# A hybrid decoder layer on one Trainium2 core: one layout for the low parts of the held weights, and two more warm-up matmuls

## The chip, the core and the metric

The kernel runs on one core of a Trainium2 chip. The core has five engines that work side by side: TensorE (matmuls; the profile calls it PE, and its weight loads PEld), VectorE (DVE), ScalarE (ACT), GpSimd (POOL) and SyncE (SP, which issues most of the DMAs). The metric is the time of one execution on the device in microseconds. Before the change it is 1077.86 us, the median of three runs (1077.21 to 1078.08).

## The reference

One decoder layer on x of 256 tokens by 2048 channels, all in float32. Cut to what carries the work:

```python
def reference(x, pre_mix_g, w_in, b_forget, sinks, grp_swa_g, grp_fox_g, w_out, post_mix_g,
              pre_ffn_g, w_up, conv_w, conv_b, w_down, post_ffn_g):
    h = rmsnorm(x, pre_mix_g)
    proj = h @ w_in                                   # 2048 -> 4368
    q_a, k_a, v_a, q_b, k_b, v_b, f_b = split(proj)
    o_a = swa_sink_attention(q_a, k_a, v_a, sinks)    # window 128, 16 heads, 2 kv heads, ALiBi
    log_f = log_sigmoid(f_b + b_forget)
    o_b = forgetting_attention(q_b, k_b, v_b, log_f)  # 16 heads, decay from cumsum(log_f)
    mix = concat([rmsnorm(o_a, grp_swa_g), rmsnorm(o_b, grp_fox_g)]) @ w_out   # 2048 -> 2048
    x = x + rmsnorm(mix, post_mix_g)
    h = rmsnorm(x, pre_ffn_g)
    u = causal_dwconv(h @ w_up, conv_w, conv_b)       # 2048 -> 2 * 5632, width 3
    gate, val = split(u)
    y = (gelu(gate) * val) @ w_down                   # 5632 -> 2048
    return x + rmsnorm(y, post_ffn_g)
```

## The kernel before

Every large product is made from split numbers. A float32 weight goes into a high part (a copy in the type that TensorE takes at full rate, `whi`, made by ScalarE on L128) and a low part (the rest, `wlo`, made by VectorE on L131); the activations are split in the same way. A product is then high by high, high by low and low by high. The activations lie transposed in `hT`: for each of 16 slices of 128 channels, 256 columns of high parts and 256 of low parts, side by side. So one matmul of a high weight with all 512 columns makes two of the three products, and a second of the low weight with the 256 high columns makes the third.

Weights come in units: a **unit** is four slices of 128 rows by 256 columns, 512 KB, loaded by one DMA of SyncE into one of five `raw` buffers, and split into one of five pairs of `whi` and `wlo` buffers (`w_parts`, `w_split`, `w_high`). The `wlo` buffer is 128 floats longer than a unit, and a held unit's low part begins at a multiple of 16 bytes inside it. Where it begins is taken from a table: `at = row[unit[0] % len(row)] * 4` floats, so 2 stands for 32 bytes, 4 for 64, 14 for 224. In the kernel before, the row is (2, 4) for everything ahead of w_up, and in the w_up projections row `LOW[place[0]]`, another one for each projection.

`proj_T` makes one projection of 256 output columns, in two banks of PSUM: 16 slices by two banks, so 32 high matmuls of 128x512 (L274) and 32 low ones of 128x256 (L281). Its runs say in which order the units go. In w_in it has four runs: units 0 and 1 high, 0 and 1 low, 2 and 3 high, 2 and 3 low; there are 11 such projections (queries and keys). In w_up it has three (LONG): units 0 and 1 high, all four low, 2 and 3 high; there are 43 of these, 21 in the first half of the feed-forward stage and 22 in the second, each half followed by its share of w_down (L296). The first gate projection of w_up is written out by itself in `first_gate`, with units that `gate_unit` splits ahead of time while the output projection still runs. Attention is woven into the w_in projections: `later(n, f)` queues its pieces, and each run's `tick()` calls those that are due.

TensorE's instructions go in the order in which they are written. The other engines' order is set by the tile framework's scheduler, save where `keep_in_program_order` or a manual schedule holds it. At the head of the program x and the first weights come in pieces: two loads of 256 KB of x, each followed by half of the first w_in unit, and then alternating units of w_in and of x. Six matmuls on a zeroed tile (`warm_up`, L183) run while the first data is under way; then a transpose of a gain vector (L189), the transposes of x's first two slices (L321, `x_part`), those of the next two, and the first matmuls of w_in (L235 high, L240 low, `unit_T`).

Of the kernel before, what the change touches and what calls it, by code (L numbers as in the profile page):

```python
# [24 lines left out]
NEG = -1e30  # L25
FHALF = 22
HOLD = 6
LOW = (
# [9 lines left out]
)  # L38
ROOM = 112


# [1 line left out]
def hybrid_layer(ctx: ExitStack, tc: tile.TileContext, x, pre_mix_g, w_in, b_forget, sinks,  # L43
# [17 lines left out]
    def bank(tag="acc"):  # L61
        return ps.tile([P, 512], F32, tag=tag, bufs=4, name="bank_" + tag)
# [4 lines left out]
    def tick():  # L67
        now[0] += 1
        for f in todo.pop(now[0], []):
            f()  # L70
# [8 lines left out]
    def w_load(src, a, c, pin=False):  # L79
        raw = wp.tile([P, UNIT], F32, tag="raw", bufs=5, name="raw")  # L80
        i = sp.dma_start(raw[:, :a * c].rearrange("p (a c) -> p a c", a=a), src)
        if pin:
            tc.keep_in_program_order(i)
        return raw, a, c

    place, unit = [-1], [0]

    def w_parts(n, keep=None, held=True):

        if keep and keep[0] is None:  # L90
            return keep[1]
        where, pre, nb = (keep[0], "h", keep[1]) if keep else (wp, "w", WB)
        hi = where.tile([P, UNIT], F32R, tag=pre + "hi", bufs=nb, name="whi")
        if where is not wp:
            lo = where.tile([P, UNIT], F32R, tag=pre + "lo", bufs=nb, name="wlo")
            return hi[:, :n], lo[:, :n]
        lo = where.tile([P, UNIT + 128], F32R, tag=pre + "lo", bufs=nb, name="wlo")
        at = 0
        if held:
            row = (2, 4) if place[0] < 0 else LOW[place[0]]  # L100
            at = row[unit[0] % len(row)] * 4
            unit[0] += 1
        return hi[:, :n], lo[:, at:at + n]

    def w_high(unit, keep=None, held=True):

        raw, a, c = unit
        n = a * c
        hi, lo = w_parts(n, keep, held)
        act.copy(hi, raw[:, :n])  # L110

        def low():
            dve.tensor_tensor(lo, raw[:, :n], hi.bitcast(F32), op=ALU.subtract)

        return [x.rearrange("p (a c) -> p a c", a=a) for x in (hi, lo)], low

    def w_split(unit, pin=False, keep=None, begun=None, between=None,
                held=True):

        raw, a, c = unit  # L120
        n = a * c
        hi, lo = begun or w_parts(n, keep, held)
        for i in range(2 if between else 1):
            cs = slice(i * 512, i * 512 + 512) if between else slice(0, n)
            if i:
                between()
            if not between or i:
                i1 = act.copy(hi[:, cs], raw[:, cs])  # L128
                if pin:
                    tc.keep_in_program_order(i1)  # L130
            i2 = dve.tensor_tensor(lo[:, cs], raw[:, cs], hi[:, cs].bitcast(F32), op=ALU.subtract)  # L131
            if pin:
                tc.keep_in_program_order(i2)
        return [x.rearrange("p (a c) -> p a c", a=a) for x in (hi, lo)]
# [4 lines left out]
    def w_rows(w, k0, a, c0, c):  # L139
        return w[k0 * P:(k0 + a) * P, c0:c0 + c].rearrange("(a p) c -> p a c", p=P)  # L140
# [40 lines left out]
    def warm_up(n):  # L181
        for i in range(n):
            pe.matmul(warm, junk[:, 0:P], junk, start=True, stop=True)  # L183
# [17 lines left out]
    def to_T(srcs, t0, n, g0, pin=False):  # L201

        for part in range(2):
            for kt, tb in srcs:
                hi = hT[:, kt, t0:t0 + n]
                gk = gcol[:, g0 + kt:g0 + kt + 1]
                if part == 0:
                    i = act.activation(hi, tb, AF.Copy, scale=gk)
                else:
                    i = dve.scalar_tensor_tensor(hT[:, kt, 256 + t0:256 + t0 + n], tb, gk,  # L210
                                                 hi.bitcast(F32), op0=ALU.mult, op1=ALU.subtract)
                if pin:
                    tc.keep_in_program_order(i)
# [43 lines left out]
    def proj_T(w, c0, banks, runs=((0, 1), (0, 1), (2, 3), (2, 3))):  # L257

        parts, last = {}, ((len(runs) - 1) % 2, KT - 1)
        unit[0] = 0  # L260
        if len(runs) == 3:
            place[0] += 1

        def get(u):
            if u not in parts:
                parts[u] = w_split(w_load(w_rows(w, u * 4, 4, c0, 256), 4, 256))
            return parts[u]

        def high(u):
            hi = get(u)[0]  # L270
            for a in range(4):
                kt = u * 4 + a
                for m, b in enumerate(banks):
                    pe.matmul(b, hi[:, a, m * P:(m + 1) * P], hT[:, kt, 0:512], start=(kt == 0),  # L274
                              stop=(last == (0, kt)))

        def low(u):
            lo = get(u)[1]
            for a in range(4):
                for m, b in enumerate(banks):  # L280
                    pe.matmul(b[:, 256:512], lo[:, a, m * P:(m + 1) * P],  # L281
                              hT[:, u * 4 + a, 0:256], start=False,
                              stop=(last == (1, u * 4 + a)))

        for n, us in enumerate(runs):
            for u in us:
                (low if n % 2 else high)(u)
                tick()
# [13 lines left out]
    with tc.tile_pool(name="mixp", bufs=1) as mp:  # L302
# [10 lines left out]
        def x_part(c, k2s, tag="att"):  # L313
            srcs = []
            for k2 in k2s:
                for j in range(2):
                    if tag == "acc" or j == 0:
                        tb = bank(tag)
                    kt = c * 4 + k2 * 2 + j
                    for t in range(2):  # L320
                        pe.transpose(tb[:, j * 256 + t * P:j * 256 + (t + 1) * P],  # L321
                                     x_in[:, t, kt * P:(kt + 1) * P], ident)
                    srcs.append((kt, tb[:, j * 256:(j + 1) * 256]))
            to_T(srcs, 0, 256, 0, True)
# [25 lines left out]


        begun = w_parts(UNIT)
        tc.keep_in_program_order(dve.tensor_copy(begun[0][:, 0:512], head[:, 0:512]))
        x_part(0, (0,), "acc")
        bkv = [bank("att"), bank("att")]
        bq0 = [bank(), bank()]
        for u in range(4):
# [244 lines left out]
        for g in range(4):  # L602
            if g == 0:
                b2 = bq0
            else:
                b2 = [bank(), bank()]
                proj_T(w_in, g * 256, b2)
            for m in range(2):
                swa_pair(2 * g + m, q_pair(b2[m]), stages(6 + 8 * (2 * g + m) - 8 * g))
# [60 lines left out]
        for g in range(4):  # L670
            bq = [bank(), bank()]
            proj_T(w_in, 1280 + g * 256, bq)
            qs = [q_pair(b) for b in bq]
            bk = [bank(), bank()]
            proj_T(w_in, 2304 + g * 256, bk)
            for m in range(2):
                ki = (2 * g + m + 2) % NK
                k_pair(bk[m], ki)
                fox_pair(2 * g + m, qs[m], ki, stages(3 + 8 * m))
# [111 lines left out]
                pieces.append(out_cols(2, 0, whole))  # L791
        gate = []

        def gate_unit(u):
            (hi, lo), low = w_high(w_load(w_rows(w_up, u * 4, 4, 0, 256), 4, 256))
            gate.extend((hi[:, i, :], lo[:, i, :]) for i in range(4))
            return low

        gate_unit(0)()
        evac_b(0, 3, out_cols(3, 0, whole))  # L800
        mix_rstd(0)
        lows = [gate_unit(u) for u in (1, 2, 3)]
        for n in range(4):
            residual(0, n)
# [254 lines left out]
```

## Time and profile before

| | |
|---|---|
| median of three runs | 1077.86 us (1077.21 to 1078.08) |
| the profiled execution | 1078.04 us |
| its span, first to last instruction | 1076.3 us |
| instructions | 16263 |
| matmuls on TensorE | 5986 |
| read from memory, written | 199.58 MB, 2.11 MB: 187 GB/s over the span |
| high matmuls of `proj_T` (L274) | 1088 + 640 |
| low matmuls of `proj_T` (L281) | 1088 + 640 |

A page of the profile gives busy time, share of the span and count for each engine, the chain of work that ended last (followed back from the last instruction, at each step to what released it), and groups of instructions with their busy time, the mean length of one in ns, and the idle time ahead of them. A row of the chain or of the timeline begins with the start in us from the beginning of the span and the length in us; `x16` at its end is the number of instructions merged into it. A matmul's record runs to the end of its drain, which overlaps the next one, so what one costs is the distance between starts.

### The profile page before, as it was taken

What the parts mean: (1) busy time and instruction counts of PE and PEld (TensorE: products, weight loads), DVE (VectorE), ACT (ScalarE), POOL (GpSimd) and SP (SyncE); (2) the same over time, 40 slices, a digit from 0 to 9 for tenths busy, and PEclk for the clock granted to TensorE, in tenths of its full rate; (3) what the DMA queues carried; (4) which work ended last, traced back from release to release, by engine and by line L of the source; (5) the groups of instructions that cost most, each with busy time, mean ns of one, the idle gap of its engine ahead of it and who ended that gap; (6) DMA issues with size and microseconds to landing.
All of it is one profiled execution on the core that took longest, in us unless ns stands there. A gap on an engine that the chain in (4) does not pass through costs nothing.

```text
span 1076.3 us, 16263 instructions
## 1 busy us (share of the span) xinstructions
PE 1064.7 (99%) x5986; PEld 927.6 (86%) x5986; DVE 735.3 (68%) x1200; ACT 613.2 (57%) x1060; POOL 225.2 (21%) x252
## 2 busy tenths in 40 slices
PE   9999999999999999999999999999999999999996
PEld 7889988888889888888888888888888888888886
DVE  5978877776568876777777444457777777765563
ACT  6766766667557755655555443446555555644450
POOL 3343333332022211212121000002121211201111
PEclk9999999999999999999999999999999999999998
DMA  8745666544863766666665666666666666665652
GB/s 282 222 123 153 181 183 204 166 160 150 296 224 110 231 195 195 193 180 197 192 187 187 198 196 194 195 193 186 185 199 186 191 193 193 192 198 190 192 169 79
DMA packets 164970, 202.88 MB, mean 188 GB/s; under 512 B 6780, under 2 KB 130972, under 8 KB 164380
## 3 DMA queue, kind: packets, MB, share of 16 engines
q1 hardware_dynamic: 164176, 201.27, 60.7%
q8 instruction: 47, 0.77, 0.3%
q10 hardware_dynamic: 716, 0.58, 0.2%
q14 instruction: 31, 0.25, 0.1%
HBM read 199.58 MB, written 2.11 MB: 187 GB/s over the span
## 4 chain that ended last, share of the span: by engine, by line
PE 95%; DVE 2%; DMA 1%; POOL 1%; ACT 1%; issue 0%; SPq 0%; DVEq 0%; POOLq 0%; ACTq 0%
PE bank_acc L296 35%; PE bank_acc L274 21%; PE bank_att L274 14%; PE bank_acc L281 11%; PE bank_att L281 7%; PE bank_att L461 1%; PE bank_att L496 1%; PE bank_att L505 1%; PE bank_att L235 1%; PE bank_acc L235 1%; DVE wlo L131 0%; PE bank_att L507 0%; DMA x_in<-in_x_dram 0%; PE bank_att L240 0%; DVE hT L754 0%; DMA cb<-c_dram 0%
## 5 line engine op out<-in xcount | busy, mean ns | idle before, releaser
L131 DVE TENSOR_TENSOR wlo<-raw,whi 128x1024 fp32r<-128x1024 f32 (+3 forms) x357 | 432.5, 1220 | 243.8 <-ACT whi L128 233.0
L128 ACT CAST whi<-raw 128x1024 fp32r<-128x1024 f32 (+3 forms) x356 | 363.6, 1034 | 274.9 <-issue 130.1
L274 PE MATMUL bank_acc<-hT,whi 128*128 128x512 f32 x1088 | 259.5, 391 | 0.0
L274 PEld LDWEIGHTS bank_acc<-hT,whi 128*128 128x128 f32 x1088 | 200.6, 188 | 39.8
L296 PE MATMUL bank_acc<-whi,G 128*128 128x512 f32 (+1 forms) x724 | 214.6, 378 | 0.0
L863 POOL TENSOR_TENSOR u<-u,rowf 128x256 f32<-128x256 f32 x88 | 97.6, 1131 | 496.7 <-DVE u L862 494.4
L296 PEld LDWEIGHTS bank_acc<-whi,G 128*128 128x128 f32 x724 | 133.7, 188 | 25.6
L274 PE MATMUL bank_att<-hT,whi 128*128 128x512 f32 x640 | 150.6, 390 | 0.0
L274 PEld LDWEIGHTS bank_att<-hT,whi 128*128 128x128 f32 x640 | 118.7, 188 | 23.9
L281 PE MATMUL bank_acc<-hT,wlo 128*128 128x256 f32 x1088 | 138.7, 281 | 0.0
L281 PEld LDWEIGHTS bank_acc<-hT,wlo 128*128 128x128 f32 x1088 | 134.8, 188 | 4.1
L296 PE MATMUL bank_acc<-wlo,G 128*128 128x512 f32 (+1 forms) x362 | 137.0, 379 | 0.0
L296 PE MATMUL bank_acc<-whi,oT 128*128 128x512 f32 (+1 forms) x272 | 82.5, 380 | 0.0
L281 PEld LDWEIGHTS bank_att<-hT,wlo 128*128 128x128 f32 x640 | 77.9, 188 | 1.7
L296 PEld LDWEIGHTS bank_acc<-wlo,G 128*128 128x128 f32 x362 | 68.1, 188 | 12.7
L281 PE MATMUL bank_att<-hT,wlo 128*128 128x256 f32 x640 | 78.3, 280 | 0.0
L296 PEld LDWEIGHTS bank_acc<-whi,oT 128*128 128x128 f32 x272 | 50.2, 188 | 9.3
L296 PE MATMUL bank_acc<-wlo,oT 128*128 128x512 f32 (+1 forms) x136 | 51.2, 377 | 0.0
L296 PE MATMUL bank_acc<-whi,hT 128*128 128x384 f32 (+1 forms) x192 | 47.6, 324 | 0.0
L865 ACT ACTIVATE yg<-u,cw 128x256 f32<-128x256 f32 x44 | 26.5, 602 | 28.8 <-POOL u L863 28.8
L865 ACT ACTIVATE yv<-u,cw 128x256 f32<-128x256 f32 x44 | 26.5, 603 | 27.0 <-POOL u L863 27.0
L479 ACT ACTIVATE p<-p,nm 128x256 f32<-128x256 f32 (+1 forms) x64 | 28.4, 445 | 20.5 <-DVE nm L467 20.4
(200 smaller groups left out, 1013.1 us busy)
## 6 DMA issues: line engine op xcount, KB each, us to landing
raw<-in_w_up_dram SPq DMA_DIRECT2D x176, 512.0 KB, 3.7
raw<-in_w_down_dram SPq DMA_DIRECT2D x88, 512.0 KB, 4.6
raw<-in_w_in_dram SPq DMA_DIRECT2D x51, 512.0 KB, 4.6
raw<-in_w_out_dram SPq DMA_DIRECT2D x32, 512.0 KB, 4.5
raw<-in_w_in_dram SPq DMA_DIRECT2D x16, 384.0 KB, 3.7
cb<-c_dram SPq DMA_DIRECT2D x8, 256.0 KB, 3.1
x_sb<-in_x_dram SPq DMA_DIRECT2D x2, 1024.0 KB
raw<-in_w_in_dram SPq DMA_DIRECT2D x5, 408.0 KB, 3.5
```

Of the source, the lines that this page charges most:

```text
L128: i1 = act.copy(hi[:, cs], raw[:, cs])
L131: i2 = dve.tensor_tensor(lo[:, cs], raw[:, cs], hi[:, cs].bitcast(F32), op=ALU.subtract)
L235: pe.matmul(b, hi[:, a, m * P:(m + 1) * P], hT[:, kt, 0:512], start=(kt == 0), stop=(kt == KT - 1))
L274: pe.matmul(b, hi[:, a, m * P:(m + 1) * P], hT[:, kt, 0:512], start=(kt == 0), stop=(last == (0, kt)))
L281: pe.matmul(b[:, 256:512], lo[:, a, m * P:(m + 1) * P], hT[:, u * 4 + a, 0:256], start=False, stop=(last == (1, u * 4 + a)))
L296: pe.matmul(b, a, r[:, cols], start=(first and i == 0), stop=(last and i == 2))
L461: pe.matmul(sb[e][:, cs], a[r, t * P:(t + 1) * P], b[r, 0:nk], start=(n == 0), stop=(n == 2))
L479: act.activation(p[:, e, cs], p[:, e, cs], AF.Exp, bias=nm[:, t, e:e + 1], scale=-1.0, accum_out=rs[:, t, e:e + 1])
L496: pe.transpose(pb[:, i * P:(i + 1) * P], p[:, e, c:c + P], ident)
L505: pe.matmul(ov, values(hl, 0), p[:, :, 0:256], start=(n == 0), stop=False)
L863: pool.tensor_tensor(u[:, 2:258], u[:, 2:258], rowf, op=ALU.mult)
L865: act.activation(y, u[:, 2:258], AF.Identity, bias=cw[:, 3, ch:ch + 1], scale=cw[:, 2, ch:ch + 1])
```

## The change

The table of 43 rows becomes one row, (14, 4, 4, 4): 224, 64, 64 and 64 bytes for the four units of every projection of three runs. Projections of four runs take the first two entries in turn: 224, 64, 224, 64. So do the units at the head of the program. Ahead of the first gate's units the count is set to zero and the period to four, so these too are at 224, 64, 64, 64 (they were at 32, 64, 32, 64). The buffers and their sizes stay, and no instruction of the splitting moves. On TensorE two more warm-up matmuls stand behind the first four transposes of x.

```diff
-LOW = (
-    (2, 0, 0, 0), (2, 1, 1, 1), (2, 2, 2, 2), (2, 3, 3, 3), (2, 4, 4, 4),
-    (2, 5, 5, 5), (2, 6, 6, 6), (2, 8, 8, 8), (2, 10, 10, 10), (2, 12, 12, 12),
-    (2, 4, 2, 4), (2, 4, 4, 2), (2, 4, 3, 4), (2, 4, 5, 4), (2, 4, 0, 4),
-    (0, 2, 2, 2), (1, 3, 3, 3), (3, 5, 5, 5), (4, 6, 6, 6), (5, 7, 7, 7),
-    (6, 8, 8, 8), (7, 9, 9, 9), (8, 10, 10, 10), (14, 16, 16, 16), (0, 4, 4, 4),
-    (1, 4, 4, 4), (3, 4, 4, 4), (5, 4, 4, 4), (6, 4, 4, 4), (8, 4, 4, 4),
-    (10, 4, 4, 4), (12, 4, 4, 4), (14, 4, 4, 4), (0, 2, 4, 6), (6, 4, 2, 0),
-    (2, 4, 6, 8), (1, 2, 3, 4), (18, 20, 18, 20), (2, 20, 2, 20), (4, 2, 4, 2),
-    (2, 6, 2, 6), (9, 11, 11, 11), (0, 1, 1, 1),
-)
+LOW = (14, 4, 4, 4)
...
-    place, unit = [-1], [0]
+    unit, period = [0], [2]
...
         if held:
-            row = (2, 4) if place[0] < 0 else LOW[place[0]]
-            at = row[unit[0] % len(row)] * 4
+            at = LOW[unit[0] % period[0]] * 4
             unit[0] += 1
...
         parts, last = {}, ((len(runs) - 1) % 2, KT - 1)
-        unit[0] = 0
-        if len(runs) == 3:
-            place[0] += 1
+        unit[0], period[0] = 0, 4 if len(runs) == 3 else 2
...
         x_part(0, (0,), "acc")
+        warm_up(2)
         bkv = [bank("att"), bank("att")]
...
         gate = []
 
+        unit[0], period[0] = 0, 4
+
         def gate_unit(u):
```

The one place where instructions move is the head of TensorE's queue. In the kernel before, the gain's transpose, the transposes of x and the first matmuls of w_in (L189, L321, L235, L240) follow each other so:

```order
L183 MATMUL bank_acc<-junk 128x512
L189 MATMUL bank_att<-ident,gpre 128x16
L321 MATMUL bank_acc<-ident,x_in 128x128 x8
L235 MATMUL bank_att<-hT,whi 128x512 x4
L240 MATMUL bank_att<-hT,wlo 128x256 x4
```

In the changed kernel the same instructions have smaller line numbers (L172 is the warm-up, L178 the gain, L308 the transposes of x, L224 and L229 the high and low matmuls):

```order
L178 MATMUL bank_att<-ident,gpre 128x16
L308 MATMUL bank_acc<-ident,x_in 128x128 x4
L172 LDWEIGHTS junk
L172 MATMUL bank_acc<-junk 128x512
L172 LDWEIGHTS junk
L172 MATMUL bank_acc<-junk 128x512
L308 MATMUL bank_acc<-ident,x_in 128x128 x4
L224 MATMUL bank_att<-hT,whi 128x512 x4
```

The eight transposes are parted in the middle, and the pair stands between; the rest of TensorE's queue and the queues of the other four engines keep their order.

## The prediction

> **What bounds the kernel now.** I read the page first, then the chain of waits, then the busy time of the engines by stretch. The page says that one engine carries the time:
>
> ```profile
> PE 1064.7 (99%) x5986; PEld 927.6 (86%) x5986; DVE 735.3 (68%) x1200; ACT 613.2 (57%) x1060; POOL 225.2 (21%) x252
> PE 95%; DVE 2%; DMA 1%; POOL 1%; ACT 1%; issue 0%; SPq 0%; DVEq 0%; POOLq 0%; ACTq 0%
> L281 PE MATMUL bank_acc<-hT,wlo 128*128 128x256 f32 x1088 | 138.7, 281 | 0.0
> L281 PE MATMUL bank_att<-hT,wlo 128*128 128x256 f32 x640 | 78.3, 280 | 0.0
> ```
>
> TensorE is 95% of the chain that ends last. The two L281 groups, 1728 matmuls, are the ones whose weights are the moved low parts. Their busy column is no price: matmuls overlap. What one costs is how much later the next one starts, and that is read from the chain.
>
> Does anything but TensorE set the pace in the w_up stage? The stretches say no:
>
> ```profile
> core 0: us, PE busy (x) PEld busy (x) DVE busy (x) ACT busy (x) POOL busy (x), PEclk, DMA share, GB/s
> ...
> 5.92:9.33 3.41, 3.33 (x12) 2.95 (x13) 2.61 (x6) 2.07 (x4) 3.28 (x5) 1.00 0.97 322
> 9.33:12.75 3.42, 3.42 (x23) 3.02 (x23) 1.64 (x3) 2.29 (x7) 2.03 (x2) 1.00 1.07 389
> ...
> 704.00:847.00 143.00, 143.00 (x832) 126.47 (x831) 101.62 (x147) 81.28 (x126) 26.64 (x24) 1.00 0.62 188
> ```
>
> From 704 to 847 us TensorE is busy for 143.00 of 143.00 us, VectorE for 101.62, the DMA engines at 0.62. A TensorE that needs 1% less has room on all sides.
>
> **The low parts in w_up.** The kernel before has a different row of LOW in each of its 43 w_up projections of three runs, so its own trace holds 43 trials of the layout, one of them the row that the change uses throughout. Row r belongs to projection r (from 0; rows 0 to 20 lie in the first half, 21 to 42 in the second), and one step in a row is 4 floats, 16 bytes. In the chain of waits each projection reads as L274 x16, L281 x32, L274 x16; neighbouring L274 runs merge to x32 where both projections write the same kind of bank. The stretch with rows 31 (12, 4, 4, 4), 32 (14, 4, 4, 4) and 33 (0, 2, 4, 6):
>
> ```profile
> 814.73 3.63 PE bank_att L274 x16
> 818.36 3.66 PE bank_att L281 x32
> 822.02 7.29 PE bank_att L274 x32
> 829.31 3.65 PE bank_att L281 x32
> 832.96 3.65 PE bank_att L274 x16
> 836.61 3.63 PE bank_acc L274 x16
> 840.24 3.78 PE bank_acc L281 x32
> ```
>
> Row 32, the change's row, needs 3.65 us for its 32 low matmuls, 114 ns each; row 33 needs 3.78. The 32 high matmuls cost 7.28 to 7.29 in each. From 814.73 to 836.61 two projections pass in 21.88 us: 10.94 each. More low runs, with what their rows say: row 4 (2, 4, 4, 4), row 16 (1, 3, 3, 3), row 23 (14, 16, 16, 16), row 24 (0, 4, 4, 4), row 27 (5, 4, 4, 4), row 28 (6, 4, 4, 4):
>
> ```profile
> 400.24 3.67 PE bank_acc L281 x32
> ...
> 532.70 3.89 PE bank_acc L281 x32
> ...
> 730.11 3.81 PE bank_att L281 x32
> 741.21 3.78 PE bank_att L281 x32
> 774.39 3.78 PE bank_att L281 x32
> 785.45 3.67 PE bank_att L281 x32
> ```
>
> The offset alone moves the run from 3.65 to 3.89 us, whatever the bank, the half or the place in the ring of five buffers. A 4 in the last three places is worth 3.65 to 3.67 behind a first unit at 2, 6, 12 or 14, and 3.78 behind a 0 or a 5: what ran just ahead counts too. So the change's row is the best of those shown, and it stood behind a projection that also ended on 4, as every projection will.
>
> Now the sum. The beginnings of the w_up runs in the chain, and of the w_down runs behind them:
>
> ```profile
> 363.34 3.63 PE bank_att L274 x16
> ...
> 584.56 119.68 PE bank_acc L296 x528
> 704.24 3.63 PE bank_acc L274 x16
> ...
> 947.06 13.15 PE bank_acc L296 x58
> ```
>
> Rows 1 to 20 take 584.56 - 363.34 = 221.22 us, rows 21 to 42 take 947.06 - 704.24 = 242.82. That is 464.04 us for 42 projections, 11.05 each. At 10.94 each they take 459.48. **Term 1: -4.56 us**, all on TensorE's path. If the pattern holds less well (3.67 for 3.65) it is -3.7.
>
> Row 0 stands in the first projection, which waits for the normalisation on its way:
>
> ```profile
> 355.40 0.56 POOL rffn L197
> ...
> 356.32 0.49 PE bank_att L223 x2
> 356.81 2.87 PE bank_acc L281 x24
> ```
>
> Up to 356.32 TensorE waits for the reciprocal root on GpSimd, so what the first gate's units and the first low unit save there is absorbed. Behind it 24 matmuls at offset 0 take 2.87 us; at 64 bytes 24 of the 32 in 3.65 would be 2.74, in 3.78 they would be 2.84. **Term 2: -0.1** (-0.03 to -0.13).
>
> **The low parts in w_in.** Eleven projections of four runs alternate (2, 4) now and (14, 4) then. Their low runs read so:
>
> ```profile
> 64.17 1.86 PE bank_acc L281 x16
> ...
> 168.14 1.85 PE bank_acc L281 x16
> ```
>
> Only the unit at 2 changes, two per projection, 22 in all. Row 4 and row 32 differ in just such a unit, 3.67 against 3.65, some 15 ns. 22 x 0.015 = 0.33 us at most, and nothing where a wait on the softmax stands behind it. **Term 3: -0.2** (0 to -0.33). VectorE writes the same 1024 floats at another start; L131's time stands in no path where TensorE is busy throughout, and would have to grow by a third to enter one.
>
> **The two warm-up matmuls.** The head of TensorE's timeline:
>
> ```profile
> 1.26 2.74 PE L183 MATMUL bank_acc<-junk 128*128 128x512 bf16 x6 [1.26 <-DVE junk L178]
> 3.93 0.28 PE L189 MATMUL bank_att<-ident,gpre 16*128 16x16 f32 x1
> 4.15 1.11 PE L321 MATMUL bank_acc<-ident,x_in 128*128 128x128 f32 x4
> 6.00 1.12 PE L321 MATMUL bank_acc<-ident,x_in 128*128 128x128 f32 x4 [0.74 <-DMA x_in<-in_x_dram]
> 6.77 2.06 PE L235 MATMUL bank_att<-hT,whi 128*128 128x512 f32 x4
> 8.62 0.96 PE L240 MATMUL bank_att<-hT,wlo 128*128 128x256 f32 x4
> 9.42 0.63 PE L235 MATMUL bank_att<-hT,whi 128*128 128x512 f32 x2
> 9.89 0.64 PE L240 MATMUL bank_att<-hT,wlo 128*128 128x256 f32 x4
> ...
> 10.83 1.03 PE L321 MATMUL bank_att<-ident,x_in 128*128 128x128 f32 x8
> ```
>
> Four transposes take 1.11 us at 4.15 and eight 1.03 at 10.83; four L240 take 0.96 at 8.62 and 0.64 at 9.89. The array ran at half speed until about 9.3 us (the clock column prints 1.00 for the stretch before too; the spacing decides). The added pair goes behind the first four transposes, into the idle 0.74 us that ends with x's arrival. At half speed one takes 2.74 / 6, under 0.46, so the pair ends at 5.26 + 0.91 = 6.17 at the latest: **a loss of 0.17 us at most**, and next to nothing, since 5.26 and 2.74 hold the drain of a last matmul that the next one overlaps.
>
> The gain is an earlier full clock. Had it come by 6 us, the 3.4 us from 6.00 to 9.42 would shrink to about 1.7 and TensorE would reach the eight transposes near 9.1. Then the next load of x is late. It is queued behind w_in's 512 KB for the first ScalarE cast below:
>
> ```profile
> 8.67 1.05 ACT L128 CAST whi<-raw 128x1024 fp32r<-128x1024 f32 x1 [0.54 <-DMA raw<-in_w_in_dram]
> ```
>
> That load landed at 8.6; another 512 KB at the stretches' 322 to 389 GB/s take 1.35 to 1.6 us, so x is there at 10.0 to 10.3. The eight transposes come 0.5 to 0.8 us earlier, no more, and as TensorE then has work to the w_up stage with few waits, the shift stays. **Term 4: -0.6** if the clock is granted a step sooner, 0 if not; bounds +0.17 and -0.8.
>
> The Trainium skill ("TensorE: Matmul & The Clock Gate", Part 1) says that the clock is released after a busy window of 3.4 us, and that the windows run free of the kernel's start. By it, a window ended at the step near 9.3, one before ran from 2.5 to 5.9 and held the idle stretch, and the pair fills that; the phase differs from run to run, which the single trace cannot show. Its Part 4 says that transposes do not count as busy; then, by an estimate from that page's window, the pair raises its busy share from about 40% to about 65%, and whether that is enough no run here shows. By the first rule term 4 is -0.6, by the second it may be 0.
>
> **The sum.** -4.56 - 0.1 - 0.2 - 0.6 = -5.46 us. The profiled execution took 1078.04 us (span 1076.3); 1078.04 - 5.46 = 1072.58. The median of the runs, 1077.86, lies 0.18 below that execution; I take 0.1 of it and forecast **1072.5 us**, 0.5% less.
>
> **The rivals.**
>
> *The layout pays, the warm-up does nothing* (0.30). Terms 1 to 3 alone: 1078.04 - 4.86 = 1073.2. For it: the step may need a whole window that two matmuls do not fill, and the head's bound may be the loads at 322 GB/s. Against it: the pair lies exactly where the idle time was.
>
> *The good state of the 4s is lost* (0.04), the slower side. Its place is the low run of each w_up projection. The row was tried once, behind (12, 4, 4, 4); the same three 4s cost 3.78 behind a 5. If a projection behind its own kind fell into that state, its low run takes 3.78. The mean low run now is 11.05 - 7.28 = 3.77; above that the change loses. 42 x 0.01 = 0.4, so 1078.4, and with the pair's 0.17 it is 1078.6; with the worst run shown, 3.89, it is 42 x 0.12 = +5.0 and 1083. Against it: rows 4, 28, 31 and 32 hold 3.65 to 3.67 on four ring phases and both kinds of bank.
>
> *The offset does not do it* (0.04). If the low runs differ by their place in the program and not by their offset, a constant row gives the mean, 11.05, and only term 4 is left: 1077.4 to 1078. The Trainium skill ("SBUF — State Buffer", Who interferes with whom) says that TensorE has independent ports for weights and moving data and never waits on anyone, which would make offsets free. By that rule, this rival; the trace disagrees, with 3.65 against 3.89 us for 32 matmuls of one shape.
>
> **How the numbers follow.** The forecast has 0.62, the rivals 0.30, 0.04 and 0.04. Runs before spread from 1077.21 to 1078.08, so 0.4 us of either sign is noise. The range of 1071.6 to 1073.7 reaches from the forecast with term 4 at -0.8 and such noise (0.9 below) to the first rival with 0.5 above it, the size of term 1's weaker case. A measurement of this kernel tells 0.2% (2.2 us) from no change. The first two cases are faster by more: 0.92. The offset without effect and the lost state at 3.78 stay within 0.2%: 0.06. Only a state as bad as 3.89 is slower: 0.02.
>
> **What would show it.** Every w_up projection's L281 x32 in the chain at 3.65 us and projections 10.94 apart; the 20 projections up to the first w_down run taking 218.8 us in place of 221.22, the 22 of the second half 240.7 in place of 242.82. The two low runs of a w_in projection together 1.84 where they are 1.85 or 1.86. L240's first four at 0.64 rather than 0.96, and the eight transposes at 10.0 to 10.3. A low run near 3.78 would refute term 1, the transposes still at 10.8 would refute term 4, and idle time of TensorE between 704 and 847 us would refute that it alone sets the pace.

## The result, and the profile after

The changed kernel takes 1072.43 us, the median of six runs (1072.0 to 1072.62), against 1077.92 us for the kernel before (six runs too, 1077.21 to 1078.08). The ratio is 0.9949, with a 95% interval of 0.9939 to 0.9959: 5.5 us or 0.5% faster, where 1072.5 us was forecast.

In the changed kernel L261 and L268 are the high and low matmuls of `proj_T` (L274 and L281 before), L283 the w_down and w_out matmuls (L296), L224 and L229 the high and low matmuls at the head (L235 and L240), L172 the warm-up, L308 the transposes of x, L117 and L120 the splits on ScalarE and VectorE. The same rows of its page:

```profile
PE 1059.5 (99%) x5988; PEld 921.6 (86%) x5988; DVE 733.6 (69%) x1200; ACT 612.7 (57%) x1060; POOL 224.1 (21%) x252
PE 95%; DVE 2%; DMA 1%; POOL 1%; ACT 1%; issue 0%; SPq 0%; DVEq 0%; POOLq 0%; ACTq 0%
L268 PE MATMUL bank_acc<-hT,wlo 128*128 128x256 f32 x1088 | 135.7, 279 | 0.0
L268 PE MATMUL bank_att<-hT,wlo 128*128 128x256 f32 x640 | 76.3, 277 | 0.0
```

The shares are what they were. TensorE's own time fell by 5.2 us and that of its weight loads by 6.0; no other engine's moved by more than 1.7. The chain of waits of the changed kernel, at the first w_up projections, where the first half ends, and over the second half (start, length, what):

```profile
32.88 3.68 PE bank_acc L261 x16
...
356.01 2.74 PE bank_acc L268 x24
358.75 3.65 PE bank_acc L261 x16
362.40 3.63 PE bank_att L261 x16
366.04 3.65 PE bank_att L268 x32
369.69 7.29 PE bank_att L261 x32
376.98 3.65 PE bank_att L268 x32
...
581.20 23.80 PE bank_acc L283 x105
...
700.88 3.63 PE bank_acc L261 x16
...
941.56 18.59 PE bank_acc L283 x82
```

Twenty projections take 581.20 - 362.40 = 218.80 us (221.22 before) and the 22 of the second half 941.56 - 700.88 = 240.68 (242.82 before). That is 459.48 us for 42, 10.94 each, and -4.56 us. TensorE is still gapless there, so nothing else became the bound:

```profile
704.00:847.00 143.00, 143.00 (x839) 126.30 (x838) 104.40 (x152) 81.40 (x128) 28.84 (x26) 1.00 0.62 191
```

The head of TensorE's timeline in the changed kernel, with the new pair as `L172 ... x2`:

```profile
4.14 1.11 PE L308 MATMUL bank_acc<-ident,x_in 128*128 128x128 f32 x4
5.05 0.96 PE L172 MATMUL bank_acc<-junk 128*128 128x512 bf16 x2
5.84 0.66 PE L308 MATMUL bank_acc<-ident,x_in 128*128 128x128 f32 x4
6.26 1.18 PE L224 MATMUL bank_att<-hT,whi 128*128 128x512 f32 x4
7.28 0.63 PE L229 MATMUL bank_att<-hT,wlo 128*128 128x256 f32 x4
8.10 0.73 PE L224 MATMUL bank_att<-hT,whi 128*128 128x512 f32 x2 [0.19 <-ACT whi L117]
8.82 0.73 PE L229 MATMUL bank_att<-hT,wlo 128*128 128x256 f32 x4
9.39 0.62 PE L224 MATMUL bank_att<-hT,whi 128*128 128x512 f32 x2
10.13 1.09 PE L308 MATMUL bank_att<-ident,x_in 128*128 128x128 f32 x8
```

The four transposes behind the pair take 0.66 us where they took 1.12, and the first four L229 0.63 where they took 0.96: full speed from just before 6 us on. The trace's own record of the granted clock has it rise at 5.77 us, where it has 9.33 in the kernel before, 3.6 us sooner. TensorE then waits, for ScalarE's cast at 8.10 and for x, whose load is now in the chain, issued at 3.33 and landed at 10.08:

```profile
3.33 6.75 DMA x_in<-in_x_dram
```

The eight transposes come at 10.13 in place of 10.83, and the first w_in projection at 32.88. Before, the chain had it at

```profile
33.58 3.68 PE bank_acc L274 x16
```

so 0.70 us came from the head and stayed.

### The profile page after: what moved, and what is told of

It is laid out like the page before. It is cut to its first block, busy times and chain, and to the rows that moved or that the text cites. A ratio compares the mean times of both kernels' runs of the same rounds, so it can differ in the third digit from the quotient of the medians.

```text
span 1070.8 us, 16266 instructions
## 1 busy us (share of the span) xinstructions
PE 1059.5 (99%) x5988; PEld 921.6 (86%) x5988; DVE 733.6 (69%) x1200; ACT 612.7 (57%) x1060; POOL 224.1 (21%) x252
## 4 chain that ended last, share of the span: by engine, by line
PE 95%; DVE 2%; DMA 1%; POOL 1%; ACT 1%; issue 0%; SPq 0%; DVEq 0%; POOLq 0%; ACTq 0%
PE bank_acc L283 35%; PE bank_acc L261 21%; PE bank_att L261 14%; PE bank_acc L268 11%; PE bank_att L268 7%; PE bank_att L449 1%; PE bank_att L484 1%; PE bank_att L493 1%; PE bank_acc L224 1%; DMA x_in<-in_x_dram 1%; PE bank_att L224 1%; DVE wlo L120 0%; PE bank_att L495 0%; DVE hT L742 0%; DMA cb<-c_dram 0%; PE bank_acc L229 0%
## 5 line engine op out<-in xcount | busy, mean ns | idle before, releaser
L120 DVE TENSOR_TENSOR wlo<-raw,whi 128x1024 fp32r<-128x1024 f32 (+3 forms) x357 | 431.1, 1216 | 240.1 <-ACT whi L117 229.7
L117 ACT CAST whi<-raw 128x1024 fp32r<-128x1024 f32 (+3 forms) x356 | 363.8, 1035 | 269.6 <-issue 125.8
L261 PE MATMUL bank_acc<-hT,whi 128*128 128x512 f32 x1088 | 259.6, 391 | 0.0
L261 PEld LDWEIGHTS bank_acc<-hT,whi 128*128 128x128 f32 x1088 | 200.5, 188 | 39.7
L283 PE MATMUL bank_acc<-whi,G 128*128 128x512 f32 (+1 forms) x724 | 214.4, 378 | 0.0
L283 PEld LDWEIGHTS bank_acc<-whi,G 128*128 128x128 f32 x724 | 133.7, 188 | 25.5
L261 PE MATMUL bank_att<-hT,whi 128*128 128x512 f32 x640 | 150.6, 390 | 0.0
L261 PEld LDWEIGHTS bank_att<-hT,whi 128*128 128x128 f32 x640 | 118.7, 188 | 23.9
L283 PE MATMUL bank_acc<-wlo,G 128*128 128x512 f32 (+1 forms) x362 | 137.0, 379 | 0.0
L268 PE MATMUL bank_acc<-hT,wlo 128*128 128x256 f32 x1088 | 135.7, 279 | 0.0
L268 PEld LDWEIGHTS bank_acc<-hT,wlo 128*128 128x128 f32 x1088 | 132.0, 188 | 4.1
L283 PE MATMUL bank_acc<-whi,oT 128*128 128x512 f32 (+1 forms) x272 | 82.5, 380 | 0.0
L283 PEld LDWEIGHTS bank_acc<-wlo,G 128*128 128x128 f32 x362 | 68.1, 188 | 12.9
L268 PEld LDWEIGHTS bank_att<-hT,wlo 128*128 128x128 f32 x640 | 76.0, 188 | 1.7
L268 PE MATMUL bank_att<-hT,wlo 128*128 128x256 f32 x640 | 76.3, 277 | 0.0
L283 PEld LDWEIGHTS bank_acc<-whi,oT 128*128 128x128 f32 x272 | 50.2, 188 | 9.2
L283 PE MATMUL bank_acc<-wlo,oT 128*128 128x512 f32 (+1 forms) x136 | 51.2, 377 | 0.0
L283 PE MATMUL bank_acc<-whi,hT 128*128 128x384 f32 (+1 forms) x192 | 47.6, 323 | 0.0
```

What stands on the lines that cost most here:

```text
L268: pe.matmul(b[:, 256:512], lo[:, a, m * P:(m + 1) * P], hT[:, u * 4 + a, 0:256], start=False, stop=(last == (1, u * 4 + a)))
L283: pe.matmul(b, a, r[:, cols], start=(first and i == 0), stop=(last and i == 2))
```

## The experiments

The theory was that the terms add up: the low parts' offsets set the low runs' time, wherever in the program they stand, and the pair brings the full clock forward. The rivals were that the place in the program and not the offset sets that time, that the early clock was the chance of one execution, and, inside the first theory, what it is that an offset is measured from.

### One part alone: the pair without the layout

```diff
 # the kernel before, with its 43 rows
         x_part(0, (0,), "acc")
+        warm_up(2)
```

> The table of 43 rows as before, and only the two more warm-up matmuls. Theory A (the parts add; the pair lets the clock rise before 6 us): the eight transposes near 10.1 us in place of 10.83, the first w_in projection 0.7 us earlier, time 1077.9 - 0.7 = 1077.2, ratio 0.9993 to 0.9995. Theory B (the earlier clock of the profile after was the phase of that execution, not the pair): the transposes at 10.8 us, 1077.9, ratio 1.000.

Measured: 1077.37 us (1076.91 to 1077.76, 11 runs) against 1077.48 for the kernel before (1076.97 to 1078.42, 15 runs), ratio 0.9998 (0.9989 to 1.0007). In time this is inconclusive: the interval holds both theories. Its timeline has the clock up early, two L183 in 0.60 us, and a wait for x:

```profile
4.99 0.60 PE L183 MATMUL bank_acc<-junk 128*128 128x512 bf16 x2
5.50 0.66 PE L321 MATMUL bank_acc<-ident,x_in 128*128 128x128 f32 x4
...
10.53 1.09 PE L321 MATMUL bank_att<-ident,x_in 128*128 128x128 f32 x8 [0.50 <-DMA x_in<-in_x_dram]
```

But the clock rose at 4.93 us, before the pair began: its two matmuls start at 4.99 and 5.21, 0.22 us apart, where the warm-up's are 0.43 apart. In this execution the pair did not bring the rise, as theory B has it. x landed 0.4 us later than in the changed kernel's profile, so the transposes gained only 0.3 us. The gain is capped by that landing, which varies.

### The other part alone: the layout without the pair

```diff
 # the changed kernel
         x_part(0, (0,), "acc")
-        warm_up(2)
```

> One layout throughout, six warm-up matmuls as before. Theory A: 42 w_up projections of 10.94 us (-4.56), w_in -0.17, the first projection -0.07, the head as before with its clock step near 9.3 us: 1077.9 - 4.8 = 1073.1, ratio 0.9955. Theory B: the same layout gain and a head that is early or late by chance, so a median near that of the changed kernel, 1072.4, with runs on both sides.

Measured: 1073.19 us (1073.01 to 1073.49), ratio 0.9958 (0.9945 to 0.9970). The forecast of theory A was 1073.1 and 0.9955. The 42 projections take 459.48 us here too, and the transposes stand at 10.8 us. That the pair was worth something was still a comparison of runs made at different times, so both were run again on one chip.

### With and without the pair, side by side

> The changed kernel once more, on the same chip as the next two, so that the pair's worth can be read from medians. Theory A (the pair brings the clock step forward to 5 to 6 us, worth what the arrival of x leaves, 0.3 to 0.75 us in the traces so far): 0.4 to 0.7 below the kernel without the pair. Theory B (chance of the phase): the same median as without the pair.

> The layout alone, six warm-up matmuls, again. Theory A: clock step near 9.3 us, the eight transposes of x at 10.8 us, ratio to the kernel before 0.9955 to 0.9960. Theory B: a step anywhere between 5 and 10 us.

Measured: with the pair 1072.62 us (1072.3 to 1072.9), without it 1073.3 (1072.48 to 1073.62): 0.68 us between the medians, with one run of the second inside the range of the first. The timeline of the one without:

```profile
5.91 1.12 PE L308 MATMUL bank_acc<-ident,x_in 128*128 128x128 f32 x4 [0.65 <-DMA x_in<-in_x_dram]
6.67 2.06 PE L224 MATMUL bank_att<-hT,whi 128*128 128x512 f32 x4
8.53 1.06 PE L229 MATMUL bank_att<-hT,wlo 128*128 128x256 f32 x4
9.38 0.96 PE L224 MATMUL bank_att<-hT,whi 128*128 128x512 f32 x2
10.18 0.63 PE L229 MATMUL bank_att<-hT,wlo 128*128 128x256 f32 x4
```

L224 and L229 run at half speed until about 10.1 us. By the traces' record the clock rose at 4.93, 5.13, 5.59, 5.77, 5.78, 6.07 and 6.22 us in the profiles of the kernels with two matmuls in the gap, seven in all (the changed kernel twice, the pair alone, and the four experiments on offsets below, which carry the pair), and at 9.30, 9.33 and 10.11 us in the three with nothing in it.

Not every one of the seven early rises is the pair's work. From rise to fall the full clock lasts 1054.718, 1058.132, 1061.545, 1064.958, 1068.372 or 1071.785 us in the twelve profiles, lengths that differ by 3.413 us or a multiple of it. So the clock changes only at moments 3.413 us apart, and where they lie differs from execution to execution. In the three without the pair such a moment came at 5.89, 5.92 and 6.69 us, and the clock did not rise; with the pair it rose at 5.77, 5.78, 6.07 and 6.22 us. For moments between 5.8 and 6.2 us, the pair decides. The rises at 4.93 (the pair alone) and 5.13 (everything 64 bytes further on, the pair 0.08 us old) owe it little or nothing. So chance has a part: a kernel without the pair may rise early in some executions, and its one run at 1072.48 us may be such a one, with no profile to show it.

What it is worth, the profiles say better than one pair of medians: the first matmul of the first w_in projection starts at 32.52 to 33.07 us in the seven, 32.80 on average, and at 33.26 to 33.56 in the three, 33.38 on average, 0.6 us later.

That the rise in the profile above came at 10.1 us and the transposes at 11.1, not near 9.3 and at 10.8, was a miss of the expectation.

### What counts as work: four transposes in place of the pair

```diff
-        warm_up(2)
+        for i in range(4):
+            pe.transpose(warm[:, i * P:(i + 1) * P], ident, ident)
```

> The changed kernel with four float32 128x128 transposes of the identity in place of the pair: about the same 0.85 us of TensorE time at half clock in the same idle stretch. If any TensorE work fills the window: the clock step at 5 to 6.3 us as with the pair, and its time. If only matmuls count, as Part 4 of the Trainium skill's page TensorE: Matmul & The Clock Gate says of transposes: the step near 9.3 us, and the time of the kernel without the pair.

Measured: 1072.48 us (1072.31 to 1072.87), ratio 0.9950 (0.9938 to 0.9963), level with the pair. Its timeline:

```profile
5.05 0.78 PE L343 MATMUL bank_acc<-ident 128*128 128x128 f32 x4
5.73 0.66 PE L308 MATMUL bank_acc<-ident,x_in 128*128 128x128 f32 x4
6.14 1.17 PE L224 MATMUL bank_att<-hT,whi 128*128 128x512 f32 x4
7.15 0.63 PE L229 MATMUL bank_att<-hT,wlo 128*128 128x256 f32 x4
```

The clock was up before 6 us, at 5.41, when the added transposes had run for 0.36 us. Whether they did it, the profile can't say. Over the 3.413 us ahead of such a moment, counted from the starts of the instructions, TensorE was at work for 92% or more of the time wherever the clock rose, and for 81% or less wherever it did not. Counting matmuls alone, without transposes, it is 53% or more and 45% or less. Either count parts the twelve profiles. The times speak for transposes: all five runs lie at or below 1072.87 us, where four of the five with nothing in the gap lie at 1073.25 or above.

### One warm-up matmul in place of two

```diff
-        warm_up(2)
+        warm_up(1)
```

> The changed kernel with one more warm-up matmul in place of two: it fills 0.43 us of the 0.95 us between the fourth transpose's slot and the next. If a window may hold some idle time: the clock step at 5 to 6.3 us as with two, and the same time within 0.2 us. If nearly the whole window has to be busy: a step near 9.3 us in the profile, and some 0.6 us more.

Measured: 1073.1 us, four runs at 1072.58, 1072.72, 1073.48 and 1073.59, ratio 0.9955 (0.9939 to 0.9972). The profile has the late rise, some 10.5 us:

```profile
5.05 0.63 PE L172 MATMUL bank_acc<-junk 128*128 128x512 bf16 x1
5.98 1.12 PE L308 MATMUL bank_acc<-ident,x_in 128*128 128x128 f32 x4 [0.30 <-DMA x_in<-in_x_dram]
6.75 2.06 PE L224 MATMUL bank_att<-hT,whi 128*128 128x512 f32 x4
```

So one was not enough in that execution, at the moment at 7.11 us, ahead of which TensorE was at work for 81% of the time; no profile with two has a moment near there, so one and two were not compared under the same conditions. The four times fall into two pairs 0.8 us apart, which is what a rise that comes early in some executions would give; with one profile that is not shown.

### The worst row throughout

```diff
-LOW = (14, 4, 4, 4)
+LOW = (1, 3, 3, 3)
```

> The changed kernel with (1, 3, 3, 3), offsets of 16, 48, 48, 48 bytes, in place of (14, 4, 4, 4). Theory A (the offset alone sets the low run): every w_up projection as row 16 of the kernel before, low run 3.89 in place of 3.65 us, projection 11.167 in place of 10.940: 42 x 0.227 = +9.5 us, and some +1 in w_in, so 1083, slower than before by 0.5%. Theory C (the low runs differ by their place in the program): projections at the mean of before, 11.05, so 1077.

Measured: 1082.82 us, ratio 1.0047 (1.0029 to 1.0065). The chain:

```profile
366.83 3.89 PE bank_att L268 x32
370.72 7.28 PE bank_att L261 x32
377.99 3.89 PE bank_att L268 x32
```

All 42 projections take 11.166 or 11.167 us, 469.00 in all. Theory A forecast 11.167; the place in the program is out as a cause. Between this row and the change's lie 469.00 - 459.48 = 9.5 us in w_up alone. In w_in, where +1 us was expected, it is 0.4 (149.66 against 149.23 for the eleven projections).

### Other rows: 43 at once

```diff
+ROWS = (
+    (14, 4, 4, 4), (4, 4, 4, 4), (7, 4, 4, 4), (9, 4, 4, 4),
...
+    (14, 4, 4, 14), (14, 4, 4, 15), (5, 4, 4, 4), (5, 4, 4, 4),
+    (0, 4, 4, 4), (0, 4, 4, 4), (14, 14, 14, 14), (12, 12, 12, 12),
...
+)
-            at = LOW[unit[0] % period[0]] * 4
+            row = ROWS[place[0]] if place[0] >= 0 and period[0] == 4 else LOW
+            at = row[unit[0] % period[0]] * 4
...
+        place[0] += len(runs) == 3
```

> The changed kernel with 43 rows again in w_up: the first unit at an offset not tried yet (4, 7, 9, 11, 13, 15 steps, then 4, 4, 4), the last unit at each other step behind (14, 4, 4), rows tried twice running, (5, 4, 4, 4) and (0, 4, 4, 4), and rows with 12, 13, 14, 15 in several places. Theory A: a row takes the same time wherever it stands, 11.066 both times for (5, 4, 4, 4) and 11.060 both times for (0, 4, 4, 4); a first unit at an odd step below 8 leaves the three 4s at 0.94 us a unit, at an even one from 2 on at 0.907. Theory D (only the row ahead decides): the second of two equal rows differs from the first. Open: whether a row below 10.94 exists; the floor would be 64 matmuls at the best rates seen, 32 x 0.2266 + 32 x 0.1133 = 10.88.

Measured: 1074.83 us, one run. From the starts of the matmuls, in us for a projection and ns for the eight low matmuls of each unit:

| row | projection | low units |
|---|---|---|
| (14, 4, 4, 12) and (14, 12, 4, 4) | 10.940 | 932, 906, 907, 907 and 932, 907, 906, 907 |
| (11, 4, 4, 4) and (13, 4, 4, 4) | 10.953 | 940, 915, 907, 907 and 934, 923, 906, 907 |
| (7, 4, 4, 4) | 10.967 | 955, 912, 907, 906 |
| (14, 4, 4, 0) | 10.994 | 932, 907, 906, 959 |
| (4, 4, 4, 4) | 11.047 | 943, 941, 943, 942 |
| (12, 12, 4, 4) | 11.046 | 942, 943, 941, 943 |
| (5, 4, 4, 4), twice | 11.066, 11.067 | 950, 943, 942, 942 |
| (0, 4, 4, 4), twice | 11.060, 11.060 | 950, 943, 942, 945 |

The rows tried twice repeat to a nanosecond or two, which is against theory D. No row lies below 10.94. Two details of the expectation were wrong: a first unit at 7 also leaves the 4s at 0.907, and one at 4 itself leaves them at 0.942. The chain shows that state in row (4, 4, 4, 4), the first run here, and the good one in (14, 4, 4, 12), the last:

```profile
365.88 3.77 PE bank_att L283 x32
...
552.62 3.65 PE bank_att L283 x32
```

(L283 is the low matmul in this kernel.) A last or a second unit at 12, 192 bytes, is as fast as one at 64. That only the place within 256 bytes counts can be read in the kernel before: its rows (2, 4, 2, 4), (18, 20, 18, 20) and (2, 20, 2, 20), which differ by 16 steps of 16 bytes in some or all places, take 10.993 us each. Why a 4 needs a unit at some other offset ahead of it, and why (12, 4, 4, 4) of the kernel before reaches the good state and (12, 12, 4, 4) does not, stays open.

### Distance or place: everything 64 bytes further on

```diff
-ROOM = 112
+ROOM = 96
...
-    const.tile([P, 112], F32, tag="room", name="room")
+    const.tile([P, 128], F32, tag="room", name="room")
```

> The changed kernel with hT, raw, whi and wlo all 64 bytes further on, so that the low parts keep their distance from hT and whi (224 and 64 bytes) but lie at 32 and 128 bytes of a 256-byte line. If the distance counts: the w_up projections stay at 10.94 and the low runs at 3.65. If the place itself counts: low units as those of row 7 of the kernel before, step 8, 0.948 to 0.956 each, low runs near 3.80 and projections at 11.07, +5.5 us. The other stages have operands whose distance changes; they may move either way.

Measured: 1075.02 us, one run. The chain at the first w_up projections, and around the first half's w_down:

```profile
366.61 3.66 PE bank_att L268 x32
370.27 7.28 PE bank_att L261 x32
377.55 3.66 PE bank_att L268 x32
...
581.77 28.38 PE bank_acc L283 x124
...
702.63 3.63 PE bank_acc L261 x16
```

The projections stay at 10.940, 459.48 us for the 42. So the distance counts and not the place. The time went up all the same: the first half's w_down takes 702.63 - 581.77 = 120.86 us where the changed kernel needs 700.88 - 581.20 = 119.68, and the second half's w_down and the stretch with the output projection are 0.7 us longer each by the starts of their matmuls. The weights of these stages moved 64 bytes against their activations, which stayed; that this is the reason was not tested by itself.

### Distance to what: the high parts moved, the low parts not

```diff
-LOW = (14, 4, 4, 4)
-ROOM = 112
+LOW = (10, 0, 0, 0)
+ROOM = 96
...
         scr = main.tile([P, 2 * D], F32, tag="y", name="scr")
+        main.tile([P, 16], F32, tag="pad", bufs=1, name="pad")
```

> The changed kernel with raw, whi and wlo 64 bytes further on, hT where it was, and (10, 0, 0, 0) as the row: the low parts lie where they lay (224, 64, 64, 64 bytes past hT's place in a 256-byte line), the high parts 64 bytes past it in place of 0. If the distance of a low part to hT, which streams against it, decides: low runs at 3.65, projections at 10.94 if the high runs stay at 7.29. If the distance of a low part to the high part decides: offsets 160, 0, 0, 0 against whi, as no row measured so far, low runs between 3.78 and 3.85 (rows 0 and 23 of the kernel before have 0.96 a unit at 0), projections 11.1.

Measured: 1083.97 us, one run. The chain:

```profile
367.83 3.67 PE bank_att L268 x32
371.50 7.46 PE bank_att L261 x32
378.96 3.67 PE bank_att L268 x32
```

The low runs stay at 3.67 us, 0.02 above the forecast and far from 3.78, the last two units at 0.907, so it is the distance of the weights to the tile that streams against them, hT, and not that to the high parts. The expectation's condition on the high runs failed, in the same sense: 64 bytes from hT in place of 0, 32 of them take 7.46 us and not 7.28, 233 ns each in place of 227. This was not a price of the change but shows that the two kinds of matmul want different distances: of the two tried, the high ones with 512 columns are faster at 0, while for the low ones with 256 no row beat 64. By what mechanism the distance sets the pace, no run shows.

## Why the prediction was right

**Term 1** (-4.56): -4.56. Reading the new layout's price off the one projection that already had it was exact, since a row's time repeats to a nanosecond: all 42 came out at 10.939 or 10.940 us. The state that the rival feared, a 4 at 0.942, exists, but behind other rows.

**Term 2** (-0.1): the 24 low matmuls behind the wait went from 2.87 to 2.74 us, the good end of its bounds; the whole first projection from 12.39 to 12.33.

**Term 3** (-0.2): the eleven w_in projections took 149.23 us in place of 149.39, -0.17. The two low runs shown in the prediction, 1.86 and 1.85 us, became 1.84, as forecast:

```profile
63.48 1.84 PE bank_acc L268 x16
...
167.37 1.84 PE bank_acc L268 x16
```

**Term 4** (-0.6): -0.70 in the profile shown, but -0.28 in the second one of the changed kernel, where x's load came later and the transposes began at 10.55. Between the means of the profiles with and without the pair it is 0.6, between the medians of the runs 0.68, and in the experiment with the pair alone 0.11, inside the noise. So -0.6 is borne out as a mean, and that the total came within 0.1 us of the forecast is in part luck. The bound was rightly placed in x's load, forecast for 10.0 to 10.3 us and landed at 10.08 here. One step on the way was wrong: TensorE was not to be ready for the transposes by 9.1 us but only near 9.9. It waited for ScalarE's cast of the first unit's second half, which waited for that half's load,

```profile
7.42 0.62 ACT L117 CAST whi<-raw 128x512 fp32r<-128x512 f32 x1 [0.32 <-DMA raw<-in_w_in_dram]
```

and then for VectorE's split behind it, until 8.82. This cast takes the same at full clock as at half (0.61 us in the kernel before). It cost nothing, since x was later still. The loss of up to 0.17 us did not come: the transposes began at 5.84, before their old 6.00.

**The range.** Its lower end was put 0.9 us below the forecast, for which the two reasons given, 0.2 and 0.4 us, make 0.6; and term 1's weaker case, -3.7 for -4.56, is 0.9 us above the forecast, not the 0.5 that was added to the first rival. The result lay so near the middle that neither mattered.

**The rivals.** The layout without the pair would have been 1073.2: measured 1073.19 and 1073.3, so this is what the kernel costs when that term is taken out. The offset without effect is refuted by the worst row's 11.167 us. The rule of the Trainium skill that was weighed there ("SBUF — State Buffer", Who interferes with whom: TensorE's ports for weights and for moving data are independent, and it never waits on anyone) would make the distance between the two free; in this trace it is not, 3.65 against 3.89 us for the same 32 matmuls. Of the Trainium skill's rules on the clock ("TensorE: Matmul & The Clock Gate"), Part 1's free-running window of 3.413 us agrees with the moments 3.413 us apart in the record of the granted clock. Part 4's, that transposes do not count as busy, is not settled here: the profiles fit it, with 53% and 45% for matmuls alone, and the times of the kernel with four transposes speak against it.

## What to carry to other kernels

When a kernel's program already holds many variants of one loop, its own trace prices each; a sum over their starts is worth more than any reasoning on what an offset does. The distance in a 256-byte line between a matmul's weights and the tile that streams against them can be worth 2% of a stage in which TensorE never waits, and moving one buffer changes that distance for every stage that uses it. Look at a gap early in the program for what it does to the clock, and for what is late behind it: here two matmuls of 0.85 us bought some 0.6 on average over the profiles, and the next load of x set the limit.

## What the runs showed that was not expected

A low run in the good state costs 113.3 ns a matmul of 256 columns, just half of the 226.6 of one with 512, and whole stretches stay at one of two rates, 113.3 or 118, for the same offset, by what ran ahead of them. The clock changes only at moments 3.413 us apart that lie elsewhere in each execution, so one profile of an early rise does not say what caused it: in the experiment with the pair alone it rose 0.06 us before the pair began. And moving everything by 64 bytes, which left the w_up projections at 10.940 us, made w_down 1% slower, 120.86 against 119.68 us.
